# Modulation of an encoder layer computed with the condition vector as the stationary operand, and gate rows placed ahead of the first head's work

## The chip, the cores and the metric

The kernel is one program on one core of one Trainium2 chip. The core's engines work side by side, each through its own list of instructions in order: PE (TensorE, matmuls; its weight loads are shown as PEld), DVE (VectorE), ACT (ScalarE), POOL (GpSimd) and SP (SyncE, which here only issues transfers). The metric is the device time of one execution in microseconds, taken as the median of several runs. A profile of one execution gives the trace.

## What is computed

A layer of a hybrid encoder is applied to two sequences, a prompt of 1024 positions and a sample of 2048, with a model width of 1024 and shared weights. A condition vector c per sequence modulates the input:

```python
mod = jax.nn.silu(c) @ w_ada + b_ada            # w_ada is 1024 x 3072
shift, scale, gate = jnp.split(mod, 3, axis=-1)
h = x * (1.0 + scale[:, None, :]) + shift[:, None, :]
z = h @ w_in                                     # 1024 x 6144, six blocks Bg Cg Va Ga Vf Gf
y_a = bg * (conv3(cg * va) + conv_b) * silu(ga)
y_f = einsum(real(fft2(vf per 128 channels)), w_fmix) * silu(gf)
o = concat(y_a, y_f) @ w_out
out = layernorm(ALPHA * x + gate * o) * ln_g + ln_b
```

The change concerns `shift`, `scale` and `gate` for both sequences, which are needed before anything else (shift and scale) and at the very end (gate).

## The kernel before

All matmuls of the projections work on fp32 values split in two fp32r parts, `hi` (a cast, made on ACT, line 88) and `lo` (source minus hi, a subtraction, line 89). `mm3` (lines 91 to 95) is a product of such pairs: hi by hi (line 93), lo by hi (line 94) and hi by lo (line 95), each with 512 moving columns. One block of w_in for one head is a tile of 128 x 8 x 128 (`wblock`, line 207), and one operand is 128 channels of h for 1024 positions (`first_operand`, line 157), so that a projection of one head is 2 halves x 8 channel blocks x 3 = 48 matmuls.

The start is written in `build` (line 829). For each of eight channel blocks i, `mods(i)` loads two pieces of w_ada, 1024 x 128 each (0.5 MB, in runs of 512 bytes), one for scale and one for shift, and computes 128 values of each for both sequences: eight fp32 matmuls per piece, with a 128 x 128 block of w_ada as the stationary operand and only two moving columns, silu(c) of the two sequences. ACT adds the bias (line 154). `first_operand(i)` then loads a block of x, turns it on PE (line 167), applies scale and shift on ACT (line 168), and splits it: the first half of the `lo` part goes to POOL, the second to DVE. In the first three rounds a block of w_in follows (`wahead`), with its `lo` part on POOL. The first head's convolution, `conv_plain` (192 matmuls), uses the operands as they come. After it come `gates`, which forms the gate rows on DVE as 2 x 8 multiply-adds over 128 x 1024 (lines 705 and 707) with w_ada's last third in eight loads, then the loading and splitting of four Vf weights, the mixing matrices (`mixers`, line 202) and the end of the gate rows (`gates_finish`, matmuls at line 725). Then `job` starts with the Vf projection of all heads (`vf_half`).

This is the order of the source. A planner of the tile framework sets the final order in each engine's list: the earlier something is written, the sooner it is placed, and some things that are ready are pulled ahead. Buffers matter as well: raw weights go through three buffers named `wst`, and a fourth load into them has to wait until the first tile has been split. SP issues its loads strictly in order, so that a load that waits for such a buffer holds everything behind it. The names used below are `big` (operands, split weights and w_ada pieces), `g` (x, h and other work tiles), `wst` (raw weights), `mm` and `aux` (PSUM banks), `mod` (scale and shift), `sc` (silu(c)), `cols` (biases) and `ident` (the identity matrix).

Of the kernel before, what the change touches and what calls it, by code (L numbers as in the profile page):

```python
# [11 lines left out]
AF = mybir.ActivationFunctionType  # L12
ALU = mybir.AluOpType
PSUM = bass.MemoryType.PSUM

P = 128
D = 1024
NK = 8
# [39 lines left out]
class Layer:  # L58
# [81 lines left out]
        self.o_d = [self.tc.dram_tile([s, D], F32, name=f"o_d{s}") for s in (1024, 2048)]  # L140
        self.ab_d = self.tc.dram_tile([NK, P, 2, P], F32, name="ab_d")

    def mods(self, i):
        nc, w = self.nc, self.h["w_ada"]
        pm = self.bank("aux")
        for s in (1, 0):
            wa = self.tl("big", [P, NK, P])
            c0 = s * D + i * P
            self.load(wa, w[0, :, c0:c0 + P].rearrange("(k p) c -> p k c", p=P))
            for k in range(NK):  # L150
                nc.tensor.matmul(pm[:, 2 * s:2 * s + 2], wa[:, k, :], self.sc[:, k, :],
                                 start=k == 0, stop=k == NK - 1)
        for s in (1, 0):
            nc.scalar.activation(self.mod[:, s, i, :], pm[:, 2 * s:2 * s + 2], AF.Identity,
                                 bias=self.cols[:, 32 + s * 8 + i:33 + s * 8 + i])

    def first_operand(self, i):
        nc = self.nc
        xs = self.tl("g", [P, NK, P])
        self.load(xs, self.h["x_prompt"][0, :, i * P:(i + 1) * P].rearrange("(t p) c -> p t c", p=P))  # L160
        hf = self.tl("g", [P, T])
        op = self.tl("big", [P, 2, T], F32R)
        for q in range(2):
            c = slice(q * 512, (q + 1) * 512)
            pt = self.bank("aux")
            for t in range(4):
                mark = nc.tensor.transpose(pt[:, t * P:(t + 1) * P], xs[:, q * 4 + t, :], self.ident)
            nc.scalar.activation(hf[:, c], pt, AF.Identity, scale=self.mod[:, 1, i, 0:1],
                                 bias=self.mod[:, 0, i, 0:1])
            self.split(op[:, 0, c], op[:, 1, c], hf[:, c], (nc.gpsimd, nc.vector)[q])  # L170
            self.marks.append(mark.ins)
        return op

# [33 lines left out]
    def wblock(self, blk, head):  # L207
        ws = self.tl("wst", [P, NK, P])
        c0 = blk * D + head * P
        self.load(ws, self.h["w_in"][0, :, c0:c0 + P].rearrange("(k p) c -> p k c", p=P))  # L210
        w = self.tl("big", [P, 2, NK, P], F32R)
        self.split(w[:, 0], w[:, 1], ws, self.nc.gpsimd if self.startup else None)
        return w

    def project(self, blk, head, ops):
# [421 lines left out]
    def job(self, seq, tok0, ops, heads, wv, ahead, **kw):  # L637
        rights = []

        def build(t):  # L640
            if t % 2 == 1 and t >= 7 and t < 15:
                rights.append(self.right(ops, (t - 7) // 2))

        plan = self.plan(heads)
        raws = [self.raw(plan[0][2])]
        self.vf_half(seq, tok0, 0, ops, wv, build)
        lefts = [self.left(*raws.pop(0))]
        raws.append(self.raw(plan[1][2]))
        y = None
        for n, (kind, j, _) in enumerate(plan):  # L650
            if n + 2 < len(plan):
                raws.append(self.raw(plan[n + 2][2]))
            if n + 1 < len(plan):
                lefts.append(self.left(*raws.pop(0)))
            else:
                wv = [self.vf_weights(1, kk) for kk in range(4)]
            left = lefts.pop(0)
            if kind == "cv":
                y = self.conv_cv(seq, tok0, j, left, rights)
            elif kind == "gb":  # L660
                self.conv_gb(seq, tok0, j, left, rights, y)
            else:
                self.gate_pair(seq, tok0, j, left, rights)
        self.vf_half(seq, tok0, 1, ops, wv, ahead(), **kw)
# [164 lines left out]
    def build(self):  # L829
# [5 lines left out]
        self.startup = True  # L835
        self.worder = [(b, 0) for b in (CG, VA, GA, BG)]
        for i in range(NK):
            self.mods(i)
            ops.append(self.first_operand(i))
            if i < 3:  # L840
                self.wahead()

        self.conv_plain(0, 0, 0, ops)
        acc = self.gates()
        wv = [self.vf_weights(0, kk) for kk in range(4)]
        self.mixers()
        self.gates_finish(acc)
# [106 lines left out]
```

## Time and profile before

| | |
|---|---|
| median of 3 runs | 2149.09 us (2148.14 to 2150.94) |
| the profiled execution | 2147.89 us |
| its span in the trace | 2146.1 us |
| PE busy | 2089.4 us, 97% |
| DVE busy | 1377.0 us, 64% |
| ACT busy | 721.5 us, 34% |
| POOL busy | 53.1 us, 2% |

The page cuts the span into 40 equal slices and gives for each the busy share of every engine and the granted TensorE clock. A matmul's entry shows its whole pass through the array, so the spacing of the starts, and not the duration, tells how fast a row of matmuls runs. Idle time is given with what ended it; idle time counts only on the engine that sets the end, and this is PE for nearly the whole span. In the trace an fp32 matmul stands as two entries, so that a piece of w_ada with eight matmuls is a row of x16.

### The profile page before, as it was taken

To read this page: it belongs to the slowest core of one execution; us is meant where nothing else is said; L and a number is where in the kernel's file an instruction comes from. 1 tells how busy PE (TensorE), PEld (TensorE's weight loads), DVE (VectorE), ACT (ScalarE), POOL (GpSimd) and SP (SyncE) were. 2 spreads that over 40 slices of the span, in tenths; PEclk is the share of its full clock that TensorE was granted. 3 is DMA by queue.
4 is the path that set the end of the run, shared out by engine and by line. 5 is a ranking of instruction groups with operands and counts; after the bars stand their busy time and mean duration, and the time that the engine had idled before them with its cause. 6 is when DMAs were issued, how large, how long until landed. Compare 5 with 4: busy or idle time off the path is not lost.

```text
span 2146.1 us, 24288 instructions
## 1 busy us (share of the span) xinstructions
PE 2089.4 (97%) x9442; PEld 1735.9 (81%) x9442; DVE 1377.0 (64%) x2279; ACT 721.5 (34%) x1046; POOL 53.1 (2%) x41
## 2 busy tenths in 40 slices
PE   7989999999999999999999999999999999699998
PEld 6868888888788888888788888888888888588887
DVE  0287555654756555564855556565576999778877
ACT  2333333332633333333533333333343433311000
POOL 2100000000000000000000000000000000011111
PEclk8999999999999999999999999999999999799999
DMA  6632222127522222229422221215666555577542
GB/s 172 183 132 69 79 89 87 61 84 125 133 82 78 79 78 70 89 69 134 124 73 77 85 89 59 89 59 173 217 208 196 180 183 185 207 247 251 172 149 103
DMA packets 342685, 269.19 MB, mean 125 GB/s; under 512 B 75239, under 2 KB 300711, under 8 KB 340394
## 3 DMA queue, kind: packets, MB, share of 16 engines
q1 hardware_dynamic: 281794, 187.37, 30.6%
q10 hardware_dynamic: 60776, 80.27, 11.6%
q8 instruction: 74, 1.21, 0.2%
q14 instruction: 41, 0.34, 0.0%
HBM read 191.05 MB, written 76.55 MB: 125 GB/s over the span
## 4 chain that ended last, share of the span: by engine, by line
PE 88%; DVE 4%; DMA 1%; ACT 1%; ACTq 1%; issue 1%; POOL 0%; DVEq 0%; SPq 0%
PE mm L95 27%; PE mm L94 27%; PE mm L93 27%; PE aux L560 2%; PE aux L93 1%; PE aux L94 1%; PE aux L95 1%; DVE big L89 1%; ACTq L85 1%; DVE big L707 1%; DMA wst<-in_w_out_dram 0%; ACT big L88 0%; ACT g L185 0%; DMA big<-vf_d 0%; DMA big<-in_x_sample_dram 0%
## 5 line engine op out<-in xcount | busy, mean ns | idle before, releaser
L93 PE MATMUL mm<-big,big 128*128 128x512 f32 (+1 forms) x2496 | 972.7, 392 | 13.8 <-ACT big L88 13.8
L94 PE MATMUL mm<-big,big 128*128 128x512 f32 (+1 forms) x2496 | 976.3, 391 | 7.3 <-POOL big L89 3.8
L95 PE MATMUL mm<-big,big 128*128 128x512 f32 (+1 forms) x2496 | 975.6, 391 | 6.7 <-DVE big L89 6.3
L93 PEld LDWEIGHTS mm<-big,big 128*128 128x128 f32 x2496 | 471.8, 189 | 113.9 <-ACT big L88 17.1
L94 PEld LDWEIGHTS mm<-big,big 128*128 128x128 f32 x2496 | 472.2, 189 | 106.4 <-POOL big L89 4.7
L95 PEld LDWEIGHTS mm<-big,big 128*128 128x128 f32 x2496 | 472.6, 189 | 105.6 <-DVE big L89 7.2
L89 DVE TENSOR_TENSOR big<-g,big 128x1024 fp32r<-128x1024 f32 (+4 forms) x244 | 234.9, 978 | 256.3 <-ACT big L88 255.7
L88 ACT CAST big<-g 128x1024 fp32r<-128x1024 f32 (+4 forms) x252 | 205.9, 833 | 417.9 <-PE mm L95 308.1
L88 ACT CAST big<-wst 128x1024 fp32r<-128x1024 f32 x150 | 155.2, 1051 | 322.4 <-PE mm L95 117.8
L89 DVE TENSOR_TENSOR big<-wst,big 128x1024 fp32r<-128x1024 f32 x147 | 177.1, 1219 | 60.8 <-ACT big L88 60.6
L308 ACT COPY e<-mm 128x512 f32<-128x512 f32 x174 | 101.8, 585 | 157.3 <-PE mm L95 155.6
L316 DVE TENSOR_TENSOR g<-mm,e 128x512 f32<-128x512 f32 x58 | 40.0, 689 | 112.8 <-PE mm L95 112.8
L257 DVE TENSOR_TENSOR g<-wst 128x512 f32<-128x512 f32 x58 | 39.8, 687 | 79.4 <-DMA wst<-in_w_in_dram 79.4
L93 PE MATMUL mm<-big,w 128*128 128x512 f32 x232 | 90.2, 389 | 0.0
L94 PE MATMUL mm<-big,w 128*128 128x512 f32 x232 | 90.2, 389 | 0.0
L95 PE MATMUL mm<-big,w 128*128 128x512 f32 x232 | 90.2, 389 | 0.0
L817 POOL TENSOR_TENSOR mv<-mv,mhalf 128x1 f32<-128x1 f32 x24 | 34.6, 1440 | 2009.3 <-DVE mv L816 2009.3
L327 DVE TENSOR_TENSOR g<-mm,e 128x512 f32<-128x512 f32 x58 | 39.9, 688 | 54.4 <-PE mm L95 54.4
L88 ACT CAST w<-wst 128x512 fp32r<-128x512 f32 x58 | 36.2, 624 | 72.3 <-PE mm L95 62.0
L809 DVE TENSOR_TENSOR g<-mm,g 128x512 f32<-128x512 f32 (+1 forms) x49 | 32.9, 676 | 36.0 <-PE mm L95 35.8
L94 PEld LDWEIGHTS mm<-big,w 128*128 128x128 f32 x232 | 43.6, 188 | 9.1
L95 PEld LDWEIGHTS mm<-big,w 128*128 128x128 f32 x232 | 43.6, 188 | 9.0
(140 smaller groups left out, 1753.7 us busy)
## 6 DMA issues: line engine op xcount, KB each, us to landing
wst<-in_w_in_dram SPq DMA_DIRECT2D x144, 512.0 KB, 3.9
wst<-y_d SPq DMA_DIRECT2D x48, 512.0 KB, 6.3
big<-in_w_ada_dram SPq DMA_DIRECT2D x24, 512.0 KB, 8.2
vf_d<-e ACTq DMA_DIRECT2D x48, 256.0 KB, 2.1
sg_d<-g ACTq DMA_DIRECT2D x24, 512.0 KB, 4.9
o_d<-e ACTq DMA_DIRECT2D x48, 256.0 KB, 2.1
g<-o_d SPq DMA_DIRECT2D x24, 512.0 KB, 3.4
out_dram<-g ACTq DMA_DIRECT2D x23, 512.0 KB, 2.7
```

The costliest lines, as they stand in the source:

```text
L88: self.nc.scalar.copy(hi, src)
L89: (eng or self.nc.vector).tensor_tensor(lo, src, hi.bitcast(F32), op=ALU.subtract)
L93: mm(out, st[0], mv[0], start=start, stop=False, **kw)
L94: mm(out, st[1], mv[0], start=False, stop=False, **kw)
L95: mm(out, st[0], mv[1], start=False, stop=stop, **kw)
L257: tt(s12[:, 0:4], a21, a22, op=ALU.add)
L308: nc.scalar.copy(e, bank)
L316: c11(lambda dst: nc.vector.tensor_tensor(dst, z, e1, op=add))
L327: c12(lambda dst: nc.vector.tensor_tensor(dst, y, e2, op=add))
L560: nc.tensor.matmul(pt[:, s * P:(s + 1) * P], vf[:, s0 + s, :], self.dft[:, s0 + s, :], start=True, stop=True)
L809: nc.vector.tensor_tensor(r[:, c], banks[q][:, 0:b - a], r[:, c], op=ALU.add)
L817: nc.gpsimd.tensor_tensor(mv[:, 2:3], mv[:, 1:2], self.mhalf, op=ALU.pow)
```

## The change

There are four edits. First, `mods` no longer takes one channel block but half of all (four blocks), and it is called twice, before operands 0 and 4. silu(c) of the two sequences is now the stationary operand (128 x 2), and w_ada streams past it, 512 columns at a time; the weights of one half and of one kind (scale or shift) come in two loads of 512 rows x 512 columns (1 MB each, in runs of 2 KB). The result is two rows of 512 values, which ACT copies out of PSUM; eight small PE transposes turn them into columns, and DVE adds the biases. Second, all splits of the start have their `lo` part on DVE, none on POOL. Third, four blocks of w_in instead of three are taken in the loop. Fourth, `gates()` is written ahead of `conv_plain`.

```diff
-    def mods(self, i):
+    def mods(self, half):
         nc, w = self.nc, self.h["w_ada"]
-        pm = self.bank("aux")
+        rows = self.tl("g", [2, 2, 512])
         for s in (1, 0):
-            wa = self.tl("big", [P, NK, P])
-            c0 = s * D + i * P
-            self.load(wa, w[0, :, c0:c0 + P].rearrange("(k p) c -> p k c", p=P))
-            for k in range(NK):
-                nc.tensor.matmul(pm[:, 2 * s:2 * s + 2], wa[:, k, :], self.sc[:, k, :],
-                                 start=k == 0, stop=k == NK - 1)
-        for s in (1, 0):
-            nc.scalar.activation(self.mod[:, s, i, :], pm[:, 2 * s:2 * s + 2], AF.Identity,
-                                 bias=self.cols[:, 32 + s * 8 + i:33 + s * 8 + i])
+            pm = self.bank("aux")
+            c0 = s * D + half * 512
+            for a in range(2):
+                wa = self.tl("big", [P, 4, 512])
+                self.load(wa, w[0, a * 512:(a + 1) * 512, c0:c0 + 512].rearrange("(k p) c -> p k c", p=P))
+                for k in range(4):
+                    nc.tensor.matmul(pm[0:2, :], self.sc[:, a * 4 + k, :], wa[:, k, :],
+                                     start=a + k == 0, stop=a * 4 + k == NK - 1)
+            nc.scalar.copy(rows[:, s, :], pm[0:2, :])
+        pt = self.bank("aux")
+        for s in range(2):
+            for i in range(4):
+                c = (s * 4 + i) * 2
+                nc.tensor.transpose(pt[:, c:c + 2], rows[:, s, i * P:(i + 1) * P], self.ident[0:2, 0:2])
+        blocks = slice(half * 4, half * 4 + 4)
+        for s in range(2):
+            bias = self.cols[:, 32 + s * 8:40 + s * 8][:, blocks].unsqueeze(2).broadcast_to([P, 4, 2])
+            nc.vector.tensor_tensor(self.mod[:, s, blocks, :],
+                                    pt[:, s * 8:s * 8 + 8].rearrange("p (i q) -> p i q", q=2), bias, op=ALU.add)
...
-            self.split(op[:, 0, c], op[:, 1, c], hf[:, c], (nc.gpsimd, nc.vector)[q])
+            self.split(op[:, 0, c], op[:, 1, c], hf[:, c])
...
-        self.split(w[:, 0], w[:, 1], ws, self.nc.gpsimd if self.startup else None)
+        self.split(w[:, 0], w[:, 1], ws)
...
         for i in range(NK):
-            self.mods(i)
+            if i % 4 == 0:
+                self.mods(i // 4)
             ops.append(self.first_operand(i))
-            if i < 3:
+            if i < 4:
                 self.wahead()
 
+        acc = self.gates()
         self.conv_plain(0, 0, 0, ops)
-        acc = self.gates()
         wv = [self.vf_weights(0, kk) for kk in range(4)]
```

What this does to the engines' lists is seen at three places. On SP, before, near the start of the list; the tiles of in_x are blocks of x, 128x8x128 from in_w_ada the pieces for scale and shift, `wst` raw weights:

```order
L82 DMA big_159<-in_w_ada_dram 128x8x128
L82 DMA big_169<-in_w_ada_dram 128x8x128
L82 DMA wst_581<-in_w_in_dram 128x8x128
L82 DMA g_229<-in_x_prompt_dram 128x8x128
L82 DMA big_207<-in_w_ada_dram 128x8x128
L82 DMA big_217<-in_w_ada_dram 128x8x128
L82 DMA wst_727<-in_w_in_dram 128x2x512
L82 DMA g_277<-in_x_prompt_dram 128x8x128
L82 DMA big_255<-in_w_ada_dram 128x8x128
L82 DMA big_265<-in_w_ada_dram 128x8x128
L82 DMA wst_732<-in_w_in_dram 128x2x512
```

On SP, now, the same part of the list, from the fourth block of x to the fifth:

```order
L82 DMA wst_245<-in_w_in_dram 128x8x128
L82 DMA g_225<-in_x_prompt_dram 128x8x128
L82 DMA wst_623<-in_w_in_dram 128x2x512
L82 DMA wst_628<-in_w_in_dram 128x2x512
L82 DMA big_252<-in_w_ada_dram 128x4x512
L82 DMA big_258<-in_w_ada_dram 128x4x512
L82 DMA big_266<-in_w_ada_dram 128x4x512
L82 DMA big_272<-in_w_ada_dram 128x4x512
L82 DMA g_290<-in_x_prompt_dram 128x8x128
L82 DMA wst_633<-in_w_in_dram 128x2x512
L82 DMA g_310<-in_x_prompt_dram 128x8x128
```

Before, each pair of w_ada pieces stood behind one `wst` load; now the four loads of the second half stand together behind wst_245, wst_623 and wst_628, which reuse the three `wst` buffers. On PE, before, one round of the start (a round of modulation, turning of x, and the first head's matmuls):

```order
L151 MATMUL aux_297<-sc,big_298 128x2 x8
L167 MATMUL aux_324<-ident,g_320 128x128 x4
L167 MATMUL aux_332<-ident,g_320 128x128 x4
L93 MATMUL mm_472<-big_280,big_155 128x512
L94 MATMUL mm_472<-big_280,big_155 128x512
L95 MATMUL mm_472<-big_280,big_155 128x512
L151 MATMUL aux_297<-sc,big_308 128x2 x8
```

On PE, now, the second half's modulation, between the first three operands' matmuls and those of the fourth (big_228):

```order
L95 MATMUL mm_516<-big_203,big_222 128x512
L154 MATMUL aux_251<-big_252,sc 2x512 x4
L154 MATMUL aux_251<-big_258,sc 2x512 x4
L154 MATMUL aux_265<-big_266,sc 2x512 x4
L154 MATMUL aux_265<-big_272,sc 2x512 x4
L161 MATMUL aux_279<-ident,g_250 128x2 x8
L178 MATMUL aux_294<-ident,g_290 128x128 x4
L178 MATMUL aux_302<-ident,g_290 128x128 x4
L93 MATMUL mm_407<-big_228,big_172 128x512
```

The modulation was spread over eight rounds; now 16 matmuls stand in one piece, ahead of matmuls whose operands are there earlier. On DVE, before, the end of the gate rows (big_693) and the first splits of the Vf weights (big_726 and on):

```order
L388 TENSOR_TENSOR g_576<-g_576,g_580 128x1024
L707 SCALAR_TENSOR_TENSOR big_693<-big_718,sc,big_693 128x1024
L707 SCALAR_TENSOR_TENSOR big_693<-big_722,sc,big_693 128x1024 x2
L89 TENSOR_TENSOR big_726<-wst_727,big_726 128x1024
L89 TENSOR_TENSOR big_731<-wst_732,big_731 128x1024
```

On DVE, now, the same place:

```order
L718 SCALAR_TENSOR_TENSOR big_371<-big_400,sc,big_371 128x1024 x2
L386 SCALAR_TENSOR_TENSOR g_511<-g_404,cols,g_511 128x1024
L89 TENSOR_TENSOR big_622<-wst_623,big_622 128x1024
L387 SCALAR_TENSOR_TENSOR g_511<-g_404,cols,g_511 128x1024
L89 TENSOR_TENSOR big_627<-wst_628,big_627 128x1024
L427 TENSOR_TENSOR g_511<-mm_568,g_511 128x512
L427 TENSOR_TENSOR g_511<-mm_593,g_511 128x512
L89 TENSOR_TENSOR big_632<-wst_633,big_632 128x1024
```

All 16 gate instructions now stand ahead of the convolution's own, and the Vf splits stand between those instead of behind them.

## Rows read from the trace of the kernel before

**Rows 1.** From the page: busy time by engine, and granted clock by slice.

```profile
PE 2089.4 (97%) x9442; PEld 1735.9 (81%) x9442; DVE 1377.0 (64%) x2279; ACT 721.5 (34%) x1046; POOL 53.1 (2%) x41
...
PEclk8999999999999999999999999999999999799999
```

**Rows 2.** Busy time in stretches: engines, granted clock, DMA share, GB/s.

```profile
25.00:30.00 5.00, 4.75 (x16) 3.64 (x16) 0.14 (x1) 3.05 (x7) 0.61 (x1) 1.00 1.05 263
30.00:35.00 5.00, 2.27 (x6) 1.54 (x7) 1.21 (x1) 0.78 (x1) 3.22 (x2) 0.83 0.14 13
...
55.00:60.00 5.00, 5.00 (x23) 4.81 (x23) 0.00 (x0) 0.00 (x0) 0.00 (x0) 0.50 1.16 307
```

**Rows 3.** The same view later, ten-microsecond stretches.

```profile
150.00:160.00 10.00, 10.00 (x46) 8.29 (x45) 10.00 (x12) 6.36 (x8) 0.00 (x0) 1.00 0.28 105
```

**Rows 4.** Timeline of the start (start, duration, engine, line, tiles, idle before).

```profile
6.73 6.98 PE L151 MATMUL aux<-sc,big 128*128 128x2 f32 x32
...
30.85 2.56 POOL L89 TENSOR_TENSOR big<-wst,big 128x1024 fp32r<-128x1024 f32 x1 [0.20 <-ACT big L88]
33.44 0.37 SPq L82 DMA_DIRECT2D wst<-in_w_in_dram  x1
...
41.63 3.41 PE L151 MATMUL aux<-sc,big 128*128 128x2 f32 x16
...
46.87 1.13 ACT L88 CAST big<-g 128x512 fp32r<-128x512 f32 x2
...
47.61 0.63 PE L93 MATMUL mm<-big,big 128*128 128x512 f32 x1
...
48.03 0.63 PE L94 MATMUL mm<-big,big 128*128 128x512 f32 x1
...
64.97 1.84 PE L151 MATMUL aux<-sc,big 128*128 128x2 f32 x16
...
66.57 0.94 PEld L167 LDWEIGHTS aux<-ident,g 128*128 128x128 f32 x8
```

**Rows 5.** Instructions by line and shape, from the start to 135 us.

```profile
L151 PE MATMUL aux<-sc,big 128*128 128x2 f32 x256 | 40.9, 291 | 3.0 <-DMA big<-in_w_ada_dram 3.0
...
L707 DVE SCALAR_TENSOR_TENSOR big<-big,sc,big 128x1024 f32<-128x1024 f32 x14 | 17.1, 1277 | 0.0
...
L168 ACT ACTIVATE g<-aux,mod 128x512 f32<-128x512 f32 x16 | 11.7, 775 | 1.0 <-PE aux L167 0.5
...
L88 ACT CAST big<-g 128x512 fp32r<-128x512 f32 x16 | 9.0, 617 | 0.0
L88 ACT CAST big<-wst 128x1024 fp32r<-128x1024 f32 x8 | 8.2, 1047 | 19.0 <-DMA wst<-in_w_in_dram 19.0
...
L89 DVE TENSOR_TENSOR big<-wst,big 128x1024 fp32r<-128x1024 f32 x5 | 5.9, 1218 | 2.6 <-ACT big L88 2.6
```

**Rows 6.** Timeline of PE where the Vf projection begins.

```profile
117.21 0.39 PE L94 MATMUL mm<-big,big 128*128 128x512 f32 x1
...
119.02 0.39 PE L94 MATMUL mm<-big,big 128*128 128x512 f32 x1
124.98 2.07 PE L95 MATMUL mm<-big,big 128*128 128x512 f32 x4 [5.57 <-DVE big L89]
...
128.95 0.40 PE L95 MATMUL mm<-big,big 128*128 128x512 f32 x1
...
130.84 3.70 PE L202 MATMUL aux<-wst,e 128*128 128x512 f32 x8 [0.58 <-DMA wst<-in_w_fmix_dram]
```

**Rows 7.** Timelines of DVE and SP at that place.

```profile
123.70 3.49 DVE L89 TENSOR_TENSOR big<-wst,big 128x1024 fp32r<-128x1024 f32 x3
...
126.09 0.38 SPq L82 DMA_DIRECT2D wst<-in_w_fmix_dram  x1
```

**Rows 8.** Two-microsecond stretches: 512-byte runs first, then the gate weights' 4 KB rows.

```profile
8.00:10.00 2.00, 2.00 (x11) 2.00 (x11) 0.00 (x0) 0.00 (x0) 0.00 (x0) 1.00 1.17 291
...
108.00:110.00 2.00, 2.00 (x11) 1.65 (x10) 2.00 (x3) 1.73 (x2) 0.00 (x0) 1.00 1.02 416
```

## The prediction

> **What bounds the kernel now.** I read the page first: PE is busy for 97% of the span, and the granted clock is below full in only a few slices, the first among them [rows 1]. Since PE sets the end nearly everywhere, only stretches in which PE idles, runs at the lower clock or does work that can be dropped are worth anything. The view by stretches then shows where: from about 140 us on PE is busy all the time at full clock [rows 3], and the change touches nothing there. Everything is decided in the first 135 us, which I read next as a timeline.
>
> Three losses stand there. (a) The modulation itself holds PE for 40.9 us [rows 5]: 16 pieces, each 1.84 us at full clock and 3.41 us in the slow stretch [rows 4], nearly all of it loading a 128 x 128 block for two moving columns. (b) SP's list is blocked by the `wst` buffers. A load into such a buffer is issued at 33.44, right behind the POOL split that begins at 30.85 and lasts 2.56 us [rows 4]; x and w_ada stand behind it, and over these five microseconds the transfers sink to 13 GB/s [rows 2]. SP's list has three such places. (c) The clock. Until about 60 us PE runs at 1.2 GHz: the head's matmuls start 0.42 us apart there, against 0.226 us at 2.4 GHz from 117.21 to 119.02 [rows 4, 6]. The granted clock is 0.50 at 55 to 60 us [rows 2], and a modulation piece takes 1.84 instead of 3.41 us from 65 us on [rows 4]. At 25 to 30 us it reads 1.00 [rows 2], but the pieces before that are as long as the slow ones (6.98 us for two, [rows 4]), so that I go by durations there. Then, at 119, PE waits 5.57 us for the first Vf split on DVE [rows 6], which stands behind the gate rows (17.1 us of multiply-adds, [rows 5]; split from 123.70, [rows 7]). PE comes back at the lower clock, until 128.95 [rows 6].
>
> I compare two marks. The first Vf matmul stands nine matmuls ahead of the one at 119.02, so at 117.0. The end of the mixing matmuls is 130.84 + 3.70 = 134.5, when 24 Vf matmuls are done.
>
> **First half of the modulation.** 40.9 us of PE work goes; 2 x 16 fp32 matmuls with 512 moving columns come. Their nearest row is that of the mixing matrices: 8 entries, that is 4 matmuls, with all starts within 3.70 us, about 0.437 us per entry or 0.875 us per matmul at full clock [rows 6]. The stationary operand is only two columns wide now, which can only make it cheaper. So 14.0 us per half at 2.4 GHz, 27 to 28 us at 1.2. PE gives up 40.9 and takes 28: the matmul time alone is worth little, and the rest of the gain must come from (b) and (c).
>
> Start: before, PE begins at 6.73 with 0.5 MB there [rows 4]; now it needs 1 MB, 0.5 MB more at 291 GB/s [rows 8], up to 8.5. I take 7.5. The other three loads (3.6 us each at that rate) come faster than PE eats them while slow. The clock: after the stall at 124.98, full-width streaming is back at 2.4 GHz after 4.0 us [rows 6], and I take this for the start too, so 2.3 matmuls by 11.5 and 13.7 x 0.875 = 12.0 us more: 23.5. Bounds: 22 with everything early, 35 if the clock stays low through all 16.
>
> Then a serial chain that was hidden in eight rounds before: ACT's copy of two rows (0.6, an estimate from its 512-column cast of 0.617, [rows 5]), eight turns (0.1 to 0.2 each; eight of x take 0.94, [rows 4]), two tiny DVE additions and the hops: 2.4 us, scale and shift at 25.9. The first operand needs on ACT 2 x 0.775, 1.13 for two casts, and 1.05 for the weight block [rows 4, 5], as ACT's list has it: 29.6, and the weight's lo part at 30.8 by DVE (1.22 instead of POOL's 2.56 us, [rows 4, 5]). So the first operand comes late, and this is paid back later.
>
> **Three operands at ACT's pace, then the second half.** Each further operand with a weight block costs ACT 1.55 + 1.1 + 1.05, some 3.6 us: the third weight block is cast at 36.8 and split at 38.1. That releases the third `wst` buffer, and only then may SP issue wst_628 and, behind it, the four loads of the second half. This is loss (b) again, once instead of three times. PE has 45 head matmuls (10 us) and turns (2 us) to fill 29.6 to 43. PE idles for some 2 us around 28, and since PE came back at the lower clock after 5.57 us of idling [rows 6], I allow 1 us here for a fall and a slow return. The first of the four loads follows 0.5 MB; 1.5 MB at 291 to 416 GB/s [rows 8] plus about 2 us: PE starts at 45. Then 14.0 us: 59.0; if all goes at 291 GB/s the fourth load lands at 56.4, and 3.5 us more make 59.9.
>
> The Trainium skill ("DMA: Bandwidth & Descriptors", Specifications) has transfers at line rate from 512 bytes on. By that, 2 KB runs would be no faster than 512-byte runs and the 59.9 would hold; the rows differ from it, with 291 against 416 GB/s for 4 KB rows [rows 8], so that I stay at 59.0.
>
> **The rest of the head.** Copy and turns: 60.8. From here PE has all operands soon enough (ACT needs 2.6 us per operand, PE 3.8) and is the bound: four turns of 0.91 and 192 - 45 = 147 matmuls x 0.226 = 33.3, together 37.0, and 0.7 for the last operand: 98.5 for the first Vf matmul, 18.5 us ahead of before.
>
> **DVE with the gate rows ahead.** The gates' 16 instructions (1.4 + 17.1 us) follow the last operand split on DVE, in the shadow of PE's last 20 us. Last split 75.9, the product of Cg and Va 78.6, the first two gate instructions and another product 80.7, 14 multiply-adds 97.6, one convolution step (1.3), Vf split at 100.1. PE has six matmuls that do not need it and arrives at 99.9. So the 5.57 us wait becomes about 0.3, and the slow clock behind it is gone. Queued behind the gate rows now are the convolution steps, for which only the store of y waits. What is late next is the mixing weights' load: it needs the second Vf split (102.6), plus the 4.75 us it took before (126.09 to 130.84, [rows 6, 7]): 107.3. PE runs dry at 105.8, waits 1.5 us, and ends the mixing at 107.3 + 3.7 = 111.0 with 31 Vf matmuls done, seven more than before. Fourth Vf weight and gate finish follow with the distances they had.
>
> **Sum.** 134.5 - 111.0 = 23.5; plus 7 x 0.226 = 1.6; minus 1.0 for the clock around 28 us: 24 us. From there PE is full in both kernels. Against the profiled execution, 2147.89 - 24 = 2123.9; the median of the runs is 1.2 above that execution, so I predict 2125. With all terms at their good or bad ends (start, 291 or 416 GB/s, clock back in 3 to 6 us, the 2 us of waits at the mixing) this case reaches from 2117 to 2131.
>
> **Rivals.**
> 1. *The clock does not rise in the first stream.* For it: before, 6.98 us of unbroken modulation matmuls from 6.73 on did not raise it [rows 4], and these have only two columns as well, now on the stationary side. Against: the moving side is now as wide as at 124.98, where it rose. Price 35 - 23.5 = 11.4: 2136.
> 2. *It neither rises in the first nor holds in the second stream.* This is the slower side. The second stream costs 13.3 more, the 45 matmuls between take 19 instead of 10 us (some 4 beyond the loads), and the return behind it 2: 11.4 + 13.3 + 4 + 2 = 31 against the 24 gained, so 2156. It decides from 25 us of loss, that is only if both streams run slow. Against it: PE enters the second stream from dense work.
> 3. *The second half's loads come late*, with SP held longer at `wst` (ACT's pace slower, a fall of the clock delaying the turns of x): PE idles before its second stream; each us of delay is one us lost, up to 8 if one more weight block comes in between: 2133.
> 4. *DVE becomes the bound at the Vf start.* From the last operand split to the Vf split DVE needs 24 us, PE 22.5; should PE be faster than I think, this caps the gain at about 26: 2123, inside the forecast.
>
> **How the numbers follow.** Forecast, with rival 4 in it, 0.67; rival 1 0.13; rival 2 0.06; rival 3 0.09; anything else 0.05. The likeliest is 2125. The range takes the forecast's 2117 to 2131 and reaches over rivals 3 and 1: 2117 to 2139, leaving out rival 2 and odd ends. A difference of 0.2% (4.3 us) is what a measurement here can tell from none. Faster: 0.67 + 0.13 + 0.09 and a little, 0.90; same 0.04; slower 0.06.
>
> **What would show it.** The profile after should have: 32 fp32 matmul entries that begin near 7.5 and narrow from 0.85 to 0.44 us of spacing near 11.5; a first head matmul at 29 to 30; the second stream from 45 to 59; the first Vf matmul near 98, with a wait for DVE under 1 us instead of 5.57; the mixing matmuls ending near 111; POOL without any split. The prediction is wrong if the streams' spacing stays at 0.85, if PE stands idle before the second stream for more than 3 us, or if the stretches behind 140 us are no longer full.

## The result, and the profile after

| | before | after |
|---|---|---|
| median | 2148.61 us (4 runs, 2145.02 to 2150.94) | 2122.52 us (4 runs, 2119.22 to 2126.48) |
| ratio to before | | 0.9881, 95% interval 0.9859 to 0.9903 |
| the profiled execution | 2147.89 us | 2122.70 us |
| its span | 2146.1 us | 2120.6 us |

The change makes the kernel faster by 26 us, and the median lies 2.5 us under the predicted 2125. From the page of the kernel after, busy time by engine and granted clock by slice:

```profile
PE 2070.9 (98%) x9266; PEld 1695.6 (80%) x9266; DVE 1380.3 (65%) x2294; ACT 720.1 (34%) x1034; POOL 35.8 (2%) x30
...
PEclk9999999999999999999999999999999999899999
```

Against [rows 1] PE is busy for 18.5 us less and the span is 25.5 us shorter; the other 7.0 us are idle time that went. The modulation's matmuls have 10.4 of the 18.5 us: 40.9 us before [rows 5], 16.65 + 13.89 = 30.5 now, as the next rows show. Little of this is matmul work: at full clock the 16 old pieces would take 16 x 1.84 = 29.4 us [rows 4], and the two streams 2 x 13.89 = 27.8. The rest of the 10.4 is time at the lower clock. The first slice of the clock, an 8 before, is a 9 now. POOL lost 11 instructions, all of them splits. The start, as a timeline of PE, ACT, DVE and SP (start, duration, engine, line, operation, tiles, idle before with what ended it):

```profile
7.54 16.65 PE L154 MATMUL aux<-big,sc 128*2 128x512 f32 x32
25.63 0.24 DVE L165 TENSOR_TENSOR mod<-aux,cols 128x8 f32<-128x8 f32 x2 [24.57 <-PE aux L161]
29.60 0.76 PE L93 MATMUL mm<-big,big 128*128 128x512 f32 x2 [1.98 <-ACT big L88]
36.17 1.06 ACT L88 CAST big<-wst 128x1024 fp32r<-128x1024 f32 x1
37.26 1.23 DVE L89 TENSOR_TENSOR big<-wst,big 128x1024 fp32r<-128x1024 f32 x1 [0.18 <-ACT big L88]
38.93 2.94 SPq L82 DMA_DIRECT2D big<-in_w_ada_dram  x4
45.26 13.89 PE L154 MATMUL aux<-big,sc 128*2 128x512 f32 x32 [1.29 <-DMA big<-in_w_ada_dram]
60.41 1.09 PE L178 MATMUL aux<-ident,g 128*128 128x128 f32 x8
```

Where 16 pieces of 1.84 to some 3.5 us stood [rows 4], two streams stand now, of 16.65 and 13.89 us. The second has no wait inside it and runs at 2.4 GHz: 16 matmuls in 13.89 us, 0.868 us each. The first loses 2.76 us against it; at 1.2 GHz half of the time is lost, so it ran slow for about 5.5 us, until 13 us. The third weight block's split ends at 38.5, and 0.4 us later SP issues the four loads of the second half, behind the `wst` load which had to wait for that split. This load, wst_628 in SP's list, brings a Vf weight, which DVE splits only at 100.36; no run here puts it behind the four. PE waits 1.29 us for the first of the four. Stretches of the same trace (us, PE, PEld, DVE, ACT and POOL busy with counts, granted clock, DMA share, GB/s):

```profile
5.00:10.00 5.00, 2.70 (x4) 0.53 (x5) 0.00 (x0) 0.36 (x2) 0.00 (x0) 1.00 1.05 393
...
30.00:35.00 5.00, 4.50 (x19) 3.47 (x18) 3.33 (x4) 4.07 (x7) 0.00 (x0) 0.66 0.59 172
...
45.00:50.00 5.00, 4.74 (x12) 0.98 (x13) 0.00 (x0) 0.00 (x0) 0.00 (x0) 1.00 1.04 390
```

From 30 to 35 us the clock was lower for a while, behind the idle time at 28. Then the place where the first head ends and the Vf projection begins, again as a timeline:

```profile
80.09 16.82 DVE L718 SCALAR_TENSOR_TENSOR big<-big,sc,big 128x1024 f32<-128x1024 f32 x14
98.03 1.21 DVE L89 TENSOR_TENSOR big<-wst,big 128x1024 fp32r<-128x1024 f32 x1
97.69 0.39 PE L93 MATMUL mm<-big,big 128*128 128x512 f32 x1
99.30 0.96 PE L95 MATMUL mm<-big,big 128*128 128x512 f32 x3
101.61 0.38 SPq L82 DMA_DIRECT2D wst<-in_w_fmix_dram  x1
105.98 3.67 PE L213 MATMUL aux<-wst,e 128*128 128x512 f32 x8 [0.71 <-DMA wst<-in_w_fmix_dram]
```

The row at 97.69 is the first Vf matmul; six matmuls later, at 99.30, stands the first that needs the Vf split of 98.03. It follows the one before it (98.82) by 0.48 us instead of 0.226: this quarter of a microsecond is what remained of the 5.57 us in [rows 6]. The mixing matmuls end at 109.65, with 31 Vf matmuls done; in the kernel before they ended at 134.5 with 24 done [rows 6]. The gain at this mark is 134.54 - 109.65 + 7 x 0.226 = 26.5 us. Further down, where both kernels wait for the next operands, it is still there. Before, and then after, at PE's next two waits for a cast:

```profile
564.27 0.50 PE L93 MATMUL mm<-big,big 128*128 128x512 f32 x1 [3.52 <-ACT big L88]
...
1038.34 0.79 PE L93 MATMUL mm<-big,big 128*128 128x512 f32 x1 [3.52 <-ACT big L88]
```

```profile
537.86 0.50 PE L93 MATMUL mm<-big,big 128*128 128x512 f32 x1 [3.52 <-ACT big L88]
...
1014.58 0.80 PE L93 MATMUL mm<-big,big 128*128 128x512 f32 x1 [4.87 <-ACT big L88]
```

The first wait, 3.52 us in both, comes 26.4 us earlier. The second has grown from 3.52 to 4.87 us, and the clock comes back later behind the first (0.66 granted from 538 to 548 us, 0.83 from 565 to 575 before): behind the second wait the same matmul comes only 23.3 us earlier. Near 1850 us, where PE waits several times in both kernels, 2 us return, and at the span's end the lead is 25.5 us.

### The profile page after: what moved, and what is told of

Same layout as the page of the kernel before. It is cut to its first block, busy times and chain, and to the rows that moved or that the text cites. A ratio compares the mean times of both kernels' runs of the same rounds, so it can differ in the third digit from the quotient of the medians.

```text
span 2120.6 us, 23891 instructions
## 1 busy us (share of the span) xinstructions
PE 2070.9 (98%) x9266; PEld 1695.6 (80%) x9266; DVE 1380.3 (65%) x2294; ACT 720.1 (34%) x1034; POOL 35.8 (2%) x30
## 4 chain that ended last, share of the span: by engine, by line
PE 89%; DVE 4%; DMA 4%; ACT 1%; issue 1%; ACTq 1%; SPq 0%; DVEq 0%
PE mm L95 27%; PE mm L94 27%; PE mm L93 27%; PE aux L571 2%; PE aux L154 1%; DMA big<-in_x_sample_dram 1%; PE aux L93 1%; PE aux L95 1%; PE aux L94 1%; DVE big L89 1%; DMA wst<-in_x_sample_dram 1%; ACT big L88 1%; DVE big L718 1%; ACTq L85 1%; DMA wst<-in_w_out_dram 0%
## 5 line engine op out<-in xcount | busy, mean ns | idle before, releaser
L93 PE MATMUL mm<-big,big 128*128 128x512 f32 (+1 forms) x2496 | 969.8, 391 | 17.1 <-ACT big L88 17.1
```

Of the source, the lines that this page charges most:

```text
L93: mm(out, st[0], mv[0], start=start, stop=False, **kw)
```

## Experiments

My theory was the prediction's: most of the gain is not the saved matmul time but the clock and the waits that go, and of the four edits the gate rows take away the wait at the Vf start. Ratios are to the kernel before, which ran beside each. A difference to the kernel after compares runs of different times; the medians of the kernel before lay between 2148.3 and 2150.0 us at these times, so 1 to 2 us of such a difference mean nothing.

### Each edit alone, in the kernel before

**gates_alone**: the gate rows ahead of the convolution, nothing else.

```
-        self.conv_plain(0, 0, 0, ops)
         acc = self.gates()
+        self.conv_plain(0, 0, 0, ops)
```

> The kernel before with one edit: the gate rows written ahead of the first head's convolution; modulation, POOL splits and three early weight blocks stay. Theory (the gate rows only pay if the fourth weight block is split before them): DVE's list now has the 16 gate instructions (18.5 us) ahead of the split of the fourth block (Bg), which PE needs near 106 us and gets near 121, so PE idles some 14 us there and comes back at the lower clock; the 5.57 us wait at the first Vf split goes. Net 5 to 9 us slower, 2154 to 2158. Rival (the order of the gate rows is a gain of its own): the 5.57 us wait and the slow clock behind it go, nothing comes instead, 7 to 9 us faster, about 2140.

Measured: 2159.28 us, ratio 1.0044 (1.0028 to 1.0059), slower, and 1.3 us more than the theory's range. The timeline of PE and DVE, from the fastest of the four executions (2153.59):

```profile
119.52 0.80 PE L94 MATMUL mm<-big,big 128*128 128x512 f32 x1 [10.60 <-DVE big L89]
...
100.31 16.82 DVE L707 SCALAR_TENSOR_TENSOR big<-big,sc,big 128x1024 f32<-128x1024 f32 x14
...
118.24 1.22 DVE L89 TENSOR_TENSOR big<-wst,big 128x1024 fp32r<-128x1024 f32 x1
```

The split that ends PE's 10.60 us of waiting stands on DVE behind the 14 multiply-adds, with one convolution step between. Here it is the split of the head's own fourth block, which this kernel takes only after the loop. The wait at the first Vf split is gone, as expected. In the full change this block is taken inside the loop, and the experiments after these three ask what that is worth.

**dve_alone**: the `lo` parts of the start on DVE.

```
-            self.split(op[:, 0, c], op[:, 1, c], hf[:, c], (nc.gpsimd, nc.vector)[q])
+            self.split(op[:, 0, c], op[:, 1, c], hf[:, c])
-        self.split(w[:, 0], w[:, 1], ws, self.nc.gpsimd if self.startup else None)
+        self.split(w[:, 0], w[:, 1], ws)
```

> The kernel before with one edit: the lo parts of the start on DVE instead of POOL. Theory: a 128x1024 split takes 1.22 instead of 2.56 us, and three times SP's blocked load into a raw weight buffer is issued that much sooner; 3 to 5 us faster, about 2144.5. Rival (the rounds are set by PE and the loads, the split is hidden): within 1 us of before.

Measured: 2143.89 us, ratio 0.9986 (0.9972 to 0.9999), with runs from 2140.0 to 2151.51: a small gain, anywhere from nothing to 6 us by the interval, so that the expected 3 to 5 us are neither confirmed nor excluded. In the profiled execution, the fastest of the nine, a modulation piece takes 1.84 us from 50.31 on, not only from 64.97 [rows 4], and the wait at the Vf start stays:

```profile
50.31 1.84 PE L151 MATMUL aux<-sc,big 128*128 128x2 f32 x16
...
117.44 2.07 PE L95 MATMUL mm<-big,big 128*128 128x512 f32 x4 [5.60 <-DVE big L89]
```

**mods_alone**: the new modulation, its two calls and the fourth block in the loop; gate rows and POOL splits as before.

```
         for i in range(NK):
-            self.mods(i)
+            if i % 4 == 0:
+                self.mods(i // 4)
             ops.append(self.first_operand(i))
-            if i < 3:
+            if i < 4:
```

> The kernel before with the new modulation and four early weight blocks alone: gate rows behind the convolution, POOL splits as before. Theory (the modulation carries the gain; the other two edits are worth some 3 and 2 us on top of it): 2127 to 2128, 20 to 21 us faster than before. Rival (the three edits share the gain about evenly): 2135 to 2140.

Measured: 2134.51 us, ratio 0.9927 (0.9912 to 0.9942). The theory's gain of 20 to 21 us did not come; the rival was nearer. PE's timeline:

```profile
48.10 13.89 PE L154 MATMUL aux<-big,sc 128*2 128x512 f32 x32 [2.38 <-DMA big<-in_w_ada_dram]
...
106.86 1.57 PE L95 MATMUL mm<-big,big 128*128 128x512 f32 x4 [3.18 <-DVE big L89]
```

So the modulation with its fourth block gives about 15 of the 26 us (12.5 to 19 by the interval). No run has the new modulation with three early blocks, so the fourth block's part in this is not shown. What it lacks against the full change is seen in both rows: the second stream starts 2.8 us later, and the wait for the Vf split is back with 3.18 us.

### The fourth block, and the gate rows on top of it

gates_alone suggested that the gate rows pay as soon as the fourth block's split stands ahead of them. These two kernels are the kernel before with `if i < 4:` in place of `if i < 3:` (**four_alone**), and with the gate rows ahead as well (**gates_four**).

> The kernel before with the fourth block of w_in taken in the loop, nothing else. The theory expects no gain by itself: the 5.57 us wait for the first Vf split stays, since that split stands behind the gate rows as before: 2147 to 2151. Rival A: the early block relieves the head's end by itself, 2143 to 2145. Rival B: one more weight block in SP's blocked list costs 4 to 6 us at the start: 2153 to 2155.

> The kernel before with gates written ahead of conv_plain and the fourth block of w_in taken in the loop; modulation and POOL splits as before. The theory (the gate rows alone lost because the split of the fourth block stood behind them on DVE, 10.60 us of PE waiting) expects that this wait is gone: DVE's first Vf split begins near 118 instead of 123.7, PE waits 1 to 2 us instead of 5.57 at the Vf start and keeps its clock, so 5 to 7 us less than before: 2142 to 2145. Rival: the gate rows only pay because the new modulation lets PE and DVE start the head earlier, or the fourth early block blocks SP once more (some 5 us): 2149 or above, with PE's wait moved to the operands of the start.

Measured: four_alone 2158.18 us, ratio 1.0046 (1.0031 to 1.0061); gates_four 2153.32 us, ratio 1.0022 (1.0009 to 1.0034). My theory missed both. Rival B of the first had the mechanism, and even it was too low; of the second the rival held. SP and PE of four_alone:

```profile
69.18 0.37 SPq L82 DMA_DIRECT2D wst<-in_w_in_dram  x1
...
76.75 2.37 PE L151 MATMUL aux<-sc,big 128*128 128x2 f32 x16 [3.50 <-DMA big<-in_w_ada_dram]
82.00 3.41 PE L151 MATMUL aux<-sc,big 128*128 128x2 f32 x16
...
106.40 0.50 PE L95 MATMUL mm<-big,big 128*128 128x512 f32 x1 [0.40 <-POOL big L89]
...
134.25 2.07 PE L95 MATMUL mm<-big,big 128*128 128x512 f32 x4 [5.98 <-DVE big L89]
```

The row of the kernel before that corresponds to 106.40:

```profile
97.54 0.50 PE L95 MATMUL mm<-big,big 128*128 128x512 f32 x1 [0.40 <-POOL big L89]
```

With the old modulation the fourth block's split makes a fourth place where SP's list stops: the next load into a `wst` buffer waits for this split until 69.18. The w_ada pieces behind it come late, PE waits 3.50 us, and the next piece takes 3.41 us: the clock has fallen to 1.2 GHz. The last operand's matmul that waits 0.40 us for POOL comes 8.9 us later than before. gates_four has the same late start, but at the Vf start:

```profile
133.14 1.24 PE L95 MATMUL mm<-big,big 128*128 128x512 f32 x3 [2.56 <-DVE big L89]
...
131.86 1.22 DVE L89 TENSOR_TENSOR big<-wst,big 128x1024 fp32r<-128x1024 f32 x1
```

The wait has gone from 5.98 to 2.56 us, and the medians of the two differ by 4.9 us, though their intervals just touch (the traces don't differ so: that of gates_four is of its longest execution, 2157.66, with a slower start). So the gate rows cost 10 us while the fourth block is late and probably bring some 5 when it is early; the early block, for its part, costs 10 us while modulation is spread over SP's list. In the full change the load that waits for the fourth block's split, wst_633, stands behind all loads of w_ada for scale and shift, with only blocks of x left to hold up. The edits hang together, and neither of these two could be judged alone.

### One edit taken back, in the kernel after

**no_gates**: `conv_plain` ahead of `gates` again.

```
-        acc = self.gates()
         self.conv_plain(0, 0, 0, ops)
+        acc = self.gates()
```

> The changed kernel with one edit undone: the gate rows are written behind the convolution again. Theory: all Vf splits then stand behind the gate rows and the convolution's steps on DVE, the first near 103.5 instead of 99.2 us; PE waits some 4 us instead of 0.1, and the mixing ends some 3 us later: 2125 to 2127, 3 to 4 us slower than the changed kernel. Rival (a third of the gain is here, as the prediction's 5.57 us plus the slow clock suggest): 8 to 9 us slower, about 2131.

Measured: 2130.76 us, ratio 0.9918 (0.9904 to 0.9933), 8.2 us over the kernel after. The rival had the size. PE's timeline, and stretches:

```profile
103.02 1.19 PE L95 MATMUL mm<-big,big 128*128 128x512 f32 x4 [3.18 <-DVE big L89]
109.33 6.64 PE L213 MATMUL aux<-wst,e 128*128 128x512 f32 x8 [2.85 <-DMA wst<-in_w_fmix_dram]
```

```profile
105.00:110.00 5.00, 2.15 (x8) 1.41 (x7) 1.46 (x2) 1.04 (x1) 0.00 (x0) 0.85 0.93 280
110.00:115.00 5.00, 5.00 (x7) 2.03 (x6) 1.22 (x1) 2.29 (x4) 0.00 (x0) 0.50 0.37 108
```

I had priced only the wait for DVE. Behind it comes a second wait, for the mixing weights, and then the granted clock is 0.50: the mixing matmuls take 6.64 instead of 3.67 us. Against the kernel after, which waits 0.25 and 0.71 us at these two places, the three are worth 2.9, 2.1 and 3.0 us, together the 8 us of the medians.

**pool_back**: the splits of the start on POOL again (the diff of dve_alone, reversed).

> The changed kernel with one edit undone: the lo parts of the start on POOL and DVE as before. Theory: the third weight block is free 1.4 us later, so that the second half's loads and PE's second stream start 1.4 us later; with the slower last operand 2 to 3 us slower than the changed kernel, 2124.5 to 2125.5. Rival (the loads come early enough): no difference, 2122.5.

Measured: 2127.22 us, ratio 0.99 (0.9885 to 0.9915), 4.7 us over the kernel after and about 2 more than expected. POOL, SP and PE, from the longest of the four executions:

```profile
38.53 2.62 POOL L89 TENSOR_TENSOR big<-wst,big 128x1024 fp32r<-128x1024 f32 x1 [0.17 <-ACT big L88]
...
41.60 2.90 SPq L82 DMA_DIRECT2D big<-in_w_ada_dram  x4
...
47.91 15.59 PE L154 MATMUL aux<-big,sc 128*2 128x512 f32 x32 [2.44 <-DMA big<-in_w_ada_dram]
```

The chain is the expected one: POOL's split ends at 41.15, the loads go out behind it 2.7 us later than in the kernel after, and PE starts its stream 2.65 us later. Only 1.4 us of this is the longer split itself (2.62 against 1.23). The rest comes from the round before: PE waits 2.14 us at 31.75 for a split on POOL, so that the turns of the third operand come late, and the third block's cast begins at 37.40 instead of 36.17. The 1.7 us by which the stream is longer is clock again. I had priced neither.

### What bounds the two streams

**stream_twice**: each matmul of the second half is made twice, and the sum halved when it is copied out.

```
                 for k in range(4):
-                    nc.tensor.matmul(pm[0:2, :], self.sc[:, a * 4 + k, :], wa[:, k, :],
-                                     start=a + k == 0, stop=a * 4 + k == NK - 1)
-            nc.scalar.copy(rows[:, s, :], pm[0:2, :])
+                    for again in range(1 + half):
+                        nc.tensor.matmul(pm[0:2, :], self.sc[:, a * 4 + k, :], wa[:, k, :],
+                                         start=a + k + again == 0, stop=a * 4 + k == NK - 1 and again == half)
+            nc.scalar.activation(rows[:, s, :], pm[0:2, :], AF.Identity, scale=1.0 / (1 + half))
```

> The changed kernel with every matmul of the second half's modulation done twice into the same sum, which is halved when it is copied out. Theory (PE sets the pace from the second stream on): 16 more fp32 matmuls of 0.875 us, the second stream lasts 28 instead of 13.9 us and everything behind it moves by 14.0 us: 2136.5. Rival (the loads of w_ada or DVE set the pace): under 8 us slower.

Measured: 2139.6 us, ratio 0.9956 (0.9942 to 0.997), 17.1 us over the kernel after.

```profile
45.93 29.32 PE L155 MATMUL aux<-big,sc 128*2 128x512 f32 x64 [2.67 <-DMA big<-in_w_ada_dram]
```

64 entries take 29.32 us, 2 x 13.89 + 1.5. PE and not the transfers bounds the second stream, and its time stands on the path. The trace is of the longest of the five executions (2144.94), but its start accounts for the gap of the medians: at the end of the mixing it is 16.3 us behind the kernel after, of which 13.9 are the second pass, 1.5 the slow clock at the stream's start and 0.7 the later start.

**warm**: three fp32 matmuls on zeros, 128 x 512, at the head of PE's list.

```
+        dull = self.tl("e", [P, 512])
+        nc.vector.memset(dull, 0.0)
+        pw = self.bank("aux")
+        for _ in range(3):
+            nc.tensor.matmul(pw, dull[:, 0:P], dull, start=True, stop=True)
```

> The changed kernel with three fp32 matmuls of 128 x 512 on zeros put at the head of PE's list, while PE waits for the first weights. Theory: of the first stream's 32 entries about six are spaced 0.85 instead of 0.44 us, 2.5 us in all; with the clock up when the stream begins it lasts 14.0 instead of 16.5 us, and all that follows moves: 2120. Rival (the loads arrive too late for a faster stream, or zeros do not raise the clock): no difference, 2122.5.

Measured: 2124.08 us, ratio 0.9878 (0.9862 to 0.9893): no gain; the rival held. PE and SP:

```profile
1.48 4.93 PE L118 MATMUL aux<-e 128*128 128x512 f32 x6 [1.48 <-DVE mhalf L848]
...
7.36 13.89 PE L159 MATMUL aux<-big,sc 128*2 128x512 f32 x32
...
26.67 0.74 PE L93 MATMUL mm<-big,big 128*128 128x512 f32 x2 [1.70 <-ACT big L88]
...
34.97 3.51 SPq L82 DMA_DIRECT2D big<-in_w_ada_dram  x4
...
43.81 15.31 PE L159 MATMUL aux<-big,sc 128*2 128x512 f32 x32 [2.96 <-DMA big<-in_w_ada_dram]
```

The first stream now runs at 2.4 GHz throughout, and the first head matmul comes 2.9 us earlier (26.67). But the second stream starts only 1.45 us earlier, after 2.96 us of waiting, and is slow at first; it ends at 59.12, and in the kernel after at 59.15. Of the 2.9 us, one half was lost at the loads and the other half, 1.4 us, at the clock behind the wait. The buffers are not to blame here: SP issues the four loads 4.0 us earlier than in the kernel after (34.97 against 38.93), but from the issue to the stream it takes 8.8 us instead of 6.3. What holds the first load so long stays open.

**weights_first**: the first three weight blocks are taken ahead of the first operand and the fourth behind it, so that the second half's loads come earlier.

```
             if i % 4 == 0:
                 self.mods(i // 4)
+                for _ in range(3 if i == 0 else 0):
+                    self.wahead()
             ops.append(self.first_operand(i))
-            if i < 4:
+            if i == 0:
                 self.wahead()
```

> The changed kernel with three weight blocks of the first head taken before the first operand and the fourth behind the first operand. Theory: ACT and DVE cast and split the blocks while PE is in the first stream, the raw buffers are free 7 us sooner, and the second half's loads are issued near 32 instead of 38.9 us; PE is the bound then and starts its second stream near 42 instead of 45.3: 3 us faster, 2119.5. Rival (x comes later behind the three raw weights that are pulled ahead, and PE starts the head later): no gain, 2122.5 or 1 to 2 us slower.

Measured: 2122.77 us, ratio 0.987 (0.9854 to 0.9887): no gain that can be told from none. PE's timeline, and a stretch:

```profile
30.26 1.94 PE L178 MATMUL aux<-ident,g 128*128 128x128 f32 x8 [4.37 <-DVE big L89]
...
45.70 13.89 PE L154 MATMUL aux<-big,sc 128*2 128x512 f32 x32
```

```profile
30.00:35.00 5.00, 4.74 (x16) 4.10 (x17) 1.46 (x3) 2.58 (x4) 0.00 (x0) 0.50 0.88 243
```

The second stream does not wait for its weights now, but PE idles 4.37 us earlier on, ahead of the turns of the second operand, and is then slow. The row names a split on DVE, which ended at 30.17; the block of x that these turns read landed at almost the same time, 30.12, after SP had issued it at 24.15 behind three raw weights (in the kernel after at 18.64). So the rival held. Of these two orders of SP's list each has one of the two waits, and one must find an order with neither.

### Both streams close together

**close_streams** puts the second half right behind the first operand: its loads then stand ahead of the first blocked `wst` load, and the stream fills the time in which ACT and DVE prepare the first operand. **close_warm** adds the diff of warm.

```
-            if i % 4 == 0:
-                self.mods(i // 4)
+            if i == 0:
+                self.mods(0)
             ops.append(self.first_operand(i))
+            if i == 0:
+                self.mods(1)
             if i < 4:
                 self.wahead()
```

> The kernel after with one thing moved: the modulation's second half stands right behind the turns of the first operand instead of behind the fourth operand. PE's list then reads stream, turns of x, stream, turns, head, and SP issues the four loads of the second half ahead of the weight block that has to wait for a wst buffer. The theory (in the kernel after the second half's loads are held behind wst, and PE stands idle twice, some 4 us before the first operand and 1.3 us before the second stream, with a slow clock around the first) expects: second stream from 25 to 39 with no idle of over 1 us, 192 matmuls of 0.226 and seven groups of turns of 0.94 behind it (50 us), first Vf matmul at 90 to 91 instead of 97.7, DVE's first Vf split near 92 to 93, the mixing ending at 102.5 to 104 instead of 109.65, so 6 to 7 us less: 2115 to 2117. Rival A: the gain is capped by DVE (24 us from the last operand split to the first Vf split, and the operands come no faster), 2119 to 2120, with a wait of 3 us or more for DVE at the Vf start. Rival B: the head then waits for ACT and its weight blocks as much as it gains, 2122 to 2123.

> The same with three 128x512 fp32 matmuls on zeros at the head of PE, as in the run warm, which brought the end of the first stream from 24.2 to 21.3. By the transfers (some 7 MB had landed by 24 us in the kernel after, and the second half's first MB is the eighth here) the second stream cannot begin before about 24, so the theory expects PE idle for 2 to 3 us ahead of it and a slow stretch, as in the run warm: a gain of 0 to 1 us over close_streams, 2114.5 to 2117. Rival: transfers are early enough, all 2.9 us come through, 2112 to 2114.

Measured: close_streams 2118.5 us (2117.49 to 2120.46), ratio 0.9857 (0.9841 to 0.9873); close_warm 2117.59 us (2116.48 to 2119.57), ratio 0.9853 (0.9838 to 0.9867). PE and DVE of close_streams:

```profile
26.42 13.89 PE L154 MATMUL aux<-big,sc 128*2 128x512 f32 x32
...
90.45 1.21 DVE L89 TENSOR_TENSOR big<-wst,big 128x1024 fp32r<-128x1024 f32 x1
...
98.72 3.59 PE L213 MATMUL aux<-wst,e 128*128 128x512 f32 x8
```

The second stream follows without a wait at full clock. DVE has its first Vf split at 90.45, and PE does not wait for it, so neither rival of close_streams shows. The mixing ends at 102.31 with 25 Vf matmuls done; six fewer than in the kernel after are worth 1.4 us, so that it is 6.0 us ahead at this place. Of these the medians keep 4.0, at least 1.5 short of what I expected; the waits for the next operands grow from 3.5 and 4.9 to 4.4 and 5.5 us in its trace. The intervals of close_streams and of the kernel after overlap a little, so this gain over the kernel after is likely rather than certain. PE of close_warm:

```profile
7.69 13.89 PE L159 MATMUL aux<-big,sc 128*2 128x512 f32 x32
...
24.74 13.89 PE L159 MATMUL aux<-big,sc 128*2 128x512 f32 x32 [0.81 <-DMA big<-in_w_ada_dram]
```

Here the transfers bound the second stream's start, as expected, but with 0.81 us of waiting where I had expected 2 to 3, and with no fall of the clock. Its 0.9 us over close_streams can't be told from none.

## Why the prediction was right, point by point

| step | predicted | measured |
|---|---|---|
| first stream begins, ends | 7.5, 23.5 | 7.54, 24.19 |
| slow at its start for | 4.0 us | about 5.5 us |
| one fp32 matmul at 2.4 GHz | 0.875 | 0.868 |
| scale and shift ready | 25.9 | 25.87 |
| first head matmul | 29.6 | 29.60 |
| third block split | 38.1 | 38.5 |
| second stream | 45 to 59 | 45.26 to 59.15 |
| last operand split | 75.9 | 75.9 |
| gate rows done | 97.6 | 96.9 |
| first Vf matmul | 98.5 | 97.69 |
| PE's wait for the Vf split | 0.3 | about 0.25 |
| PE's wait for the mixing weights | 1.5 | 0.71 |
| mixing ends | 111.0 | 109.65 |

- **The modulation.** The row of the mixing matmuls [rows 6] carried over to a stationary operand two columns wide: 0.868 against 0.875. Bound by PE, as stream_twice shows, it could be summed without the transfers. That scale and shift were ready at 25.87 is partly luck: the stream ended 0.7 us later than summed, and the copy, turns and additions behind it took 1.7 us instead of 2.4.
- **The clock.** Rivals 1 and 2 fall: the first stream rises to 2.4 GHz by itself, the second holds it. (Rival 1's price, 35 - 23.5, is 11.5 and not 11.4; its 2136 stays.) The stall at 124.98 in [rows 6] served as measure for the return, 4.0 us; in the profiled execution it took 1.5 us more. Other traces lie on both sides: the same first stream takes 15.69 in weights_first and 16.11 in stream_twice, which means 3.6 and 4.4 us. A return after a stall in dense work was a loose measure for a start, and no row of before could have given a better one.
- **SP's list.** Named as loss (b), it set the second stream's start within 0.3 us, by one path: third cast, third split, `wst` load, w_ada loads. Rival 3 did not come, but pool_back and warm show how near it was: with loads that leave 2.7 us later, or a head that starts 2.9 us earlier, PE waits 2.4 to 3.0 us there.
- **The allowance of 1.0 us** for the clock around 28 us was not needed. The clock did fall, 0.66 was granted from 30 to 35 us, but PE waits for the second half's loads at 44 in any case. At most the 0.4 us by which the third split was late can be its doing.
- **DVE.** The 24 us from the last operand split to the end of the Vf split were 23.3 (75.9 to 99.24), and PE's 22.5 to its first Vf matmul were 21.8. Rival 4 was close but didn't decide.
- **What was mis-sized.** At the mark I had 24 us and the trace 26.5. The terms: PE was at the Vf start 0.8 us earlier than summed (half of it already at the turns behind the second stream, 60.41 against 60.8), and the mixing weights' load took 4.37 us instead of the 4.75 of before [rows 6, 7] and was issued 1.0 us earlier, so that the wait was half; and the clock's 1.0 us did not come off. The 1 us that the span keeps less than the mark is lost later, at waits for the next operands. The prediction did not have these ("From there PE is full in both kernels"), and its reading that PE is busy at full clock from 140 us on was wrong already for the kernel before: [rows 3] show only ten microseconds, and in the same trace PE waits 3.52 us at 564 and at 1038.
- **The transfers.** The first loads moved at 393 GB/s, the second half's at 390, with a DMA share of 1.05 and 1.04, against 291 with a share of 1.17 for 512-byte runs [rows 8]. The Trainium skill ("DMA: Bandwidth & Descriptors", Specifications) has transfers at line rate from 512 bytes on, which does not agree with these rows; the measurement decides. It moved little here: PE takes 13.89 / 4 = 3.5 us for a load of 1 MB, which lands in 2.7 us at 390 GB/s and would land in 3.6 us at 291.
- **What the prediction did not see** is how the edits lean on each other. It priced the fourth block and the gate rows inside one sum, which is right for this kernel; priced one by one against the kernel before, both would have been wrong in sign.

## What to carry to other kernels

Where a product has few rows and large weights, let the weights stream and keep the few rows stationary: here 16 weight pieces, between which PE waited and stayed slow until 60 us, became two streams, of which the first brought the clock up and the second ran at 2.4 GHz throughout. When loads share one queue in strict order, follow each of them back to the buffer that it or the load ahead of it waits for; this path set the start of the second stream in the kernel after, no_gates, mods_alone and pool_back, where PE had the first load 6.1 to 6.3 us after its issue. It is not the whole story: in stream_twice and warm it took 7.7 and 8.8 us. An edit that takes away one wait is to be tried with what stands queued behind it on every engine: the same move of the gate rows cost 10 us or brought some 5 to 8, by where one weight block's split stood.

## What the runs showed of the hardware that I had not expected

- After three matmuls on zeros, 4.93 us at the head of PE, the stream at 7.36 in warm ran at 2.4 GHz from its first entry (13.89 us). After two modulation pieces of the old form, 6.98 us without a break, PE was still slow [rows 4]: a later piece took 3.41 us, twice the 1.84 at full clock.
- A short wait of PE costs clock in some traces only. Ahead of the second stream PE waited 1.29 us in the kernel after, 2.38 in mods_alone, and the stream took 13.89; it waited 2.44 us in pool_back, 2.67 in stream_twice and 2.96 in warm, and the stream lost 1.4 to 1.7 us. 2.38 and 2.44 us lie too close to call it a matter of the wait's length alone; what else decides stays open.
- The granted clock reads 1.00 from 5 to 10 us in the kernel after, while its stream's length says that it ran slow there, as in the kernel before at 25 to 30 us [rows 2]. The first clock record of the trace stands at 13.1 us after and at 30.0 us before, and the view counts time without a record as 1.00, so that ahead of these marks durations are the only witness.
